# Up projection of a hybrid decoder layer: four split weights before the last operands, and the first step's products ordered by half of the tokens

## The chip, the cores and the metric

The kernel runs on one core of a Trainium2 chip. The metric is device time in microseconds (us) of one execution. The engines are named as in the profile: PE is TensorE (PEld its weight loads), DVE is VectorE, ACT is ScalarE, POOL is GpSimd and SP is SyncE; ACT, POOL and SP also issue the transfers of their own DMA queues. A row of the timeline gives the start in us from the start of the span, the duration, the engine, the line of the kernel, the operation, output<-inputs and the shape; in brackets stands the idle time of the engine before it and what ended that.

## The reference, cut to what matters

One layer: two mixers (retention, and windowed attention with sinks) on a common input projection, an output projection with a residual, and a squared-ReLU MLP with a residual. All of it is float32.

```python
D_MODEL = 1024
D_FF = 4 * D_MODEL
def rms_norm(x, gain=None):
    xf = x.astype(jnp.float32)
    y = xf * lax.rsqrt(jnp.mean(xf * xf, axis=-1, keepdims=True) + EPS)
    if gain is not None:
        y = y * gain.astype(jnp.float32)
    return y.astype(x.dtype)
```

There are 1024 prompt tokens and 8 x 8 decode tokens, 1088 in all. The change lies where the output projection ends and the MLP's first product, `rms_norm(y, gain) @ w_up`, begins; the norm's factor of each token is left out of the product and multiplied in afterwards, ahead of the square.

## The kernel before, in words

**Tokens and numbers.** The 1088 tokens stand in two superchunks s = 0, 1 of two halves of Q = 272 columns. A float32 number is split into a high part (a cast by ACT, L754) and a low part (source less high part, a subtraction by DVE, L755). A product of two split matrices is three matmuls (`mm3`, L177 to L180): high by high (L178), low weight by high operand (L179), high weight by low operand (L180). PE works in the order in which its instructions are written, and so do the other engines.

**Products.** The up projection goes in 16 steps `up(fp)`. Each step is a 2 x 2 block product by seven multiplications, in the order `PROD = (1, 2, 6, 5, 7, 4, 3)`. Product i needs a weight `w_i` and an operand, for each superchunk: 12 matmuls of 128 x 272 for each pair (i, s), so 24 for a product. Weights 1, 2 and 4 are pieces of the raw weights, weights 5, 6, 7 and 3 are sums that POOL makes (`comb`, L971). In the rows `op0` is the operand of product 1, `op1` of product 2, `op3` of 5, `op4` of 6, `op5` of 7, `op6` of 4 and `op2` of 3; `op4_1h` is the high part of product 6's operand for superchunk 1. The profile leaves such numbers out: there `op_1h` is the high part of any operand of superchunk 1, `wu_w` any split weight, `wu_s` any sum and `wu_r` any raw half. The results go to PSUM banks: products 1, 6, 7 and 4 to `psx`, 2 to `psy`, 5 and 3 to `psz`, one bank for each superchunk.

**Weights.** `left` (L961 to L981) loads the raw weights of a step as two transfers of 512 KB, `r1` and `r2`, on ACT's queue (L769) into a ring "raw" of three buffers; it yields the split weights one by one (`wsplit`), and makes the sums when it comes to a product that needs them. A transfer into a ring buffer waits until the buffer's readers are done.

**The end of the output projection.** `residual(1, m)` (L798) handles row block m of superchunk 1: POOL loads a part of the input (L800), DVE adds the two projection banks (L802), POOL stores y (L804), DVE multiplies with the gain to give f (L810), ACT squares y (L816), and DVE adds the square to the sum of squares `acc` (L817). `operands(1, m)` (L830) then makes the operands of the block: for m of 4 and above POOL makes three combinations (L845, L847, L849), and each of five operands is split by ACT and DVE. The last two blocks are m = 6 and 7. Before them the code takes the first two weights of step 0 (`ready`); so the rows of DVE and ACT hold the splits of weights 1 and 2 ahead of the operands of block 6 and 7.

**The norm of superchunk 1.** `norm(1)` (L853) sums the squares over partitions on PE (48 small matmuls into `psr`), scales them on DVE (L860, tile `nsinks`) and takes the root on POOL (L132). `norm_spread(1)` (L863) spreads the factors over partitions on PE (`psn`, L868), and ACT copies them to `rsf` (L872). In step 0 it comes after product 2 and product 6.

**After a product.** ACT copies a finished `psx` bank (L1046); after product 2 DVE adds `psy` (L1028), scales and clips (`act`, L1033), and ACT squares (L1034). A bank is written again only when its copy is done. The order of the instructions on an engine is not that of the code: a scheduler of the framework moves instructions by its own estimate of when they can run. The lists of the section on the change are the result of it.

## Time and profile before

| | |
|---|---|
| median of three runs | 1242.56 us (1240.81 to 1243.02) |
| the profiled execution's own time | 1242.26 us |
| its span, first to last instruction | 1240.5 us |
| mean granted TensorE clock | 0.983 |
| busy PE, DVE, POOL, ACT | 96%, 68%, 45%, 41% of the span |

The profiled execution has 1.8 us around its span. PE is busy nearly throughout, so what counts is where it isn't. The stage of this case lies between 525 us, where the output projection of superchunk 1 comes to its last blocks, and 572 us, where the second step of the up projection is under way. The granted clock of PE is given as a share of full speed, in ten-us stretches here.

### The profile page before, as it was taken

Reading aid. Unit: us, or ns where it says so; the run is one execution under the profiler, and the core shown is the slowest. Engines: PE = TensorE matmul, PEld = TensorE weight load, DVE = VectorE, ACT = ScalarE, POOL = GpSimd, SP = SyncE. Lnnn points to the kernel's source line nnn. Section 1 sums busy time; section 2 is a strip of 40 time slices with the busy share of each in tenths; the row PEclk is TensorE's granted clock in tenths of the full one; section 3 lists DMA queues with packets and bytes.
Section 4 is the critical chain, followed back from the end, with each engine's and each line's share of the span. In section 5 each row is a group of like instructions: output and inputs, shape, how many; then the busy total and the mean of one; then the engine's idle time right before and its main releaser. Section 6 shows DMA issues by size and latency. Waiting matters only on the chain.

```text
span 1240.5 us, 23936 instructions
## 1 busy us (share of the span) xinstructions
PE 1197.0 (96%) x9621; PEld 1150.0 (93%) x9621; DVE 849.0 (68%) x1508; ACT 507.3 (41%) x1035; POOL 557.5 (45%) x463
## 2 busy tenths in 40 slices
PE   7999999999998999969999999999899999999998
PEld 5999888888888999869999999999899999999998
DVE  7856667643136888787767666666568778897776
ACT  6343434673123435444444444444453423233331
POOL 8425333323225646467666666666662231253000
PEclk9999999999899999979999999999999999999999
DMA  6211225232415653523444444444575445643215
GB/s 236 70 59 59 88 98 165 91 101 76 120 52 183 212 163 121 164 82 125 141 141 142 151 142 150 142 151 165 178 260 162 146 150 175 202 166 126 73 55 180
DMA packets 102277, 169.46 MB, mean 137 GB/s; under 512 B 11999, under 2 KB 68255, under 8 KB 101911
## 3 DMA queue, kind: packets, MB, share of 16 engines
q1 hardware_dynamic: 88279, 123.24, 29.6%
q10 hardware_dynamic: 11328, 35.79, 8.9%
q0 software_dynamic: 2560, 8.91, 2.3%
q8 instruction: 75, 1.23, 0.4%
q14 instruction: 35, 0.29, 0.1%
HBM read 114.30 MB, written 53.61 MB: 135 GB/s over the span
## 4 chain that ended last, share of the span: by engine, by line
PE 56%; DVE 6%; DMA 2%; issue 2%; POOL 1%; ACT 1%; ACTq 0%; DVEq 0%; POOLq 0%; SPq 0%
PE psd L179 8%; PE psd L180 8%; PE psd L178 8%; PE psx L178 5%; PE psx L179 5%; PE psx L180 5%; PE psz L178 3%; PE psz L180 3%; PE psz L179 3%; PE pso L178 2%; PE pso L180 1%; PE pso L179 1%; PE psy L178 1%; PE psy L180 1%; PE psy L179 1%
## 5 line engine op out<-in xcount | busy, mean ns | idle before, releaser
L178 PE MATMUL psd<-uh,wd_w 128*128 128x272 f32 x896 | 259.5, 290 | 5.3 <-ACT a L1161 5.2
L180 PE MATMUL psd<-ul,wd_w 128*128 128x272 f32 x896 | 259.1, 290 | 2.2 <-DVE ul L755 2.2
L179 PE MATMUL psd<-uh,wd_w 128*128 128x272 f32 x896 | 260.5, 291 | 0.4 <-DVE wd_w L755 0.4
L178 PEld LDWEIGHTS psd<-uh,wd_w 128*128 128x128 f32 x896 | 170.3, 190 | 5.8 <-ACT a L1161 5.7
L180 PEld LDWEIGHTS psd<-ul,wd_w 128*128 128x128 f32 x896 | 169.7, 190 | 2.7 <-DVE ul L755 2.6
L179 PEld LDWEIGHTS psd<-uh,wd_w 128*128 128x128 f32 x896 | 169.7, 189 | 0.9 <-DVE wd_w L755 0.9
L1163 DVE TENSOR_TENSOR a<-a,psd 128x272 f32<-128x272 f32 x248 | 101.2, 429 | 41.7 <-PE psd L180 41.7
L755 DVE TENSOR_TENSOR wu_w<-wu_s,wu_w 128x512 fp32r<-128x512 f32 x64 | 58.7, 921 | 52.6 <-ACT wu_w L754 51.5
L754 ACT CAST wd_w<-wd_s 128x512 fp32r<-128x512 f32 x64 | 37.4, 619 | 118.4 <-PE psd L180 103.4
L755 DVE TENSOR_TENSOR ul<-ur,uh 128x1088 fp32r<-128x1088 f32 x56 | 81.6, 1485 | 5.6 <-ACT uh L754 5.6
L178 PE MATMUL psx<-op_0h,wu_w 128*128 128x272 f32 x256 | 74.9, 292 | 5.2 <-ACT wu_w L754 5.2
L178 PE MATMUL psx<-op_1h,wu_w 128*128 128x272 f32 x256 | 74.7, 292 | 0.0
L180 PE MATMUL psx<-op_1l,wu_w 128*128 128x272 f32 x256 | 74.6, 292 | 0.0
L180 PE MATMUL psx<-op_0l,wu_w 128*128 128x272 f32 x256 | 74.6, 292 | 0.0
L179 PE MATMUL psx<-op_0h,wu_w 128*128 128x272 f32 x256 | 74.4, 291 | 0.0
L179 PE MATMUL psx<-op_1h,wu_w 128*128 128x272 f32 x256 | 74.3, 290 | 0.0
L1033 DVE SCALAR_TENSOR_TENSOR m<-m,rsf 128x272 f32<-128x272 f32 x96 | 70.6, 736 | 4.6 <-ACT rsf L872 2.0
L366 POOL TENSOR_TENSOR sp<-sp,ssp 128x1024 f32<-128x1024 f32 (+1 forms) x16 | 28.6, 1787 | 100.4 <-DVE ssp L365 95.7
L754 ACT CAST uh<-ur 128x1088 fp32r<-128x1088 f32 x56 | 59.6, 1099 | 15.0 <-PE psd L179 9.1
L1074 POOL TENSOR_TENSOR r4t<-r3t,r4t 128x272 f32<-128x272 f32 x64 | 64.3, 1014 | 1.2
L178 PE MATMUL psf<-hnh,wqk_hi 128*128 128x384 f32 (+1 forms) x192 | 63.3, 330 | 0.0
L180 PE MATMUL psf<-hnl,wqk_hi 128*128 128x384 f32 (+1 forms) x192 | 63.1, 329 | 0.0
(328 smaller groups left out, 3797.0 us busy)
## 6 DMA issues: line engine op xcount, KB each, us to landing
ur<-u_d SPq DMA_DIRECT2D x52, 544.0 KB, 4.9
u_d<-r4t SPq DMA_DIRECT2D x32, 544.0 KB, 4.6
wu_r<-in_w_up ACTq DMA_DIRECT2D x32, 512.0 KB, 4.2
wd_r<-in_w_down ACTq DMA_DIRECT2D x30, 512.0 KB, 5.6
u_d<-r3t SPq DMA_DIRECT2D x32, 408.0 KB, 3.0
y<-in_xY POOLq DMA_DIRECT2D x16, 272.0 KB, 3.2
y_d<-y POOLq DMA_DIRECT2D x16, 272.0 KB, 3.6
yt<-y_d SPq DMA_DIRECT2D x16, 272.0 KB, 3.6
```

The source lines that it names most:

```text
L178: nc.tensor.matmul(ps, lh, rh, start=first, stop=False, skip_group_check=more)
L179: nc.tensor.matmul(ps, ll, rh, start=False, stop=False, skip_group_check=more)
L180: nc.tensor.matmul(ps, lh, rl, start=False, stop=last, skip_group_check=more)
L366: nc.gpsimd.tensor_tensor(s, s, ss.unsqueeze(2).broadcast_to([P, 4, n]), ALU.mult)
L754: nc.scalar.copy(hi, src)
L755: lo_eng.tensor_tensor(lo, src, hi.bitcast(F32), ALU.subtract)
L1033: nc.vector.scalar_tensor_tensor(t_, src, 0.0, rsf[:, s, h, :], ALU.max, ALU.mult)
L1074: sub = lambda o_, p_, q_: nc.gpsimd.tensor_tensor(o_, p_, q_, ALU.subtract)
L1163: nc.vector.tensor_tensor(to, to, ps, ALU.add)
```

## The change

Four things are changed, all at the passage from the output projection to the up projection.

1. The two sums for weights 5 and 6 of step 0 are made before the last two row blocks, in a buffer `wu0_s56` of the ring "raw", not in the pool of sums. Four weights (1, 2, 6, 5) are taken ahead of the last operands, not two; weights 6 and 5 go to other buffers (tag "wa").
2. `residual` no longer adds up the squares itself: it returns a function that does it, and for superchunk 1 this is called after the operands of the block.
3. Step 0 works its first products in the order 1 and 1 (for s = 0 and 1), then 2, 6, 5 for s = 0, then 2, 6, 5 for s = 1; the later products stay.
4. `norm(1)` is called after product 5 of s = 0, and `norm_spread(1)` after product 5 of s = 1, its matmuls behind that product's last matmul by `issue_after`. For superchunk 0 they are bound to the output projection's last matmul so far.

The diff, without the lines of `up` that are only indented in another way:

```diff
     def mm3(ps, lh, ll, rh, rl, first, last, more=False):
...
-        nc.tensor.matmul(ps, lh, rl, start=False, stop=last, skip_group_check=more)
+        return nc.tensor.matmul(ps, lh, rl, start=False, stop=last, skip_group_check=more)
...
         nc.vector.tensor_scalar(f, y, g_ffn[:, m : m + 1], None, ALU.mult)
-        if m == 0:
-            acc[s] = mw.tile([P, 2, Q], F32, tag="acc", name=f"acc{s}")
-            nc.scalar.activation(acc[s], y, AF.Square)
-        else:
-            sq = om.tile([P, 2, Q], F32, tag="sq", name=f"sq{s}_{m}")
-            nc.scalar.activation(sq, y, AF.Square)
-            nc.vector.tensor_tensor(acc[s], acc[s], sq, ALU.add)
+
+        def squares():
+            if m == 0:
+                acc[s] = mw.tile([P, 2, Q], F32, tag="acc", name=f"acc{s}")
+                nc.scalar.activation(acc[s], y, AF.Square)
+            else:
+                sq = om.tile([P, 2, Q], F32, tag="sq", name=f"sq{s}_{m}")
+                nc.scalar.activation(sq, y, AF.Square)
+                nc.vector.tensor_tensor(acc[s], acc[s], sq, ALU.add)
+
+        return squares
...
-    def norm_spread(s):
+    def norm_spread(s, ins):
...
+                with tc.issue_after(ins.ins):
+                    nc.tensor.matmul(
...
         if ms == (6, 7):
-            gen0 = left(PROD, a["w_up"][0], "wu0", nc.vector, tags=("wa", "wa", "wb", "wb"))
-            ready = [next(gen0), next(gen0)]
+            r0 = [rawload(a["w_up"][0][:, i * 1024 : i * 1024 + 1024], f"wu0_r{i + 1}") for i in range(2)]
+            s56 = mw.tile([P, 1024], F32, tag="raw", name="wu0_s56", bufs=3)
+            nc.gpsimd.tensor_tensor(s56[:, :512], r0[1][:, :512], r0[1][:, 512:], ALU.add)
+            nc.gpsimd.tensor_tensor(s56[:, 512:], s56[:, :512], r0[0][:, :512], ALU.subtract)
+            gen0 = left(
+                PROD, None, "wu0", nc.vector, tags=("wa", "wa", "wa", "wa", "wb", "wb", "wb"), raws=r0,
+                sums={5: s56[:, :512], 6: s56[:, 512:]})
+            ready = [next(gen0) for _ in range(4)]
         for m in ms:
-            residual(1, m, [pss[m, h] for h in range(2)])
+            squares = residual(1, m, [pss[m, h] for h in range(2)])
             if rest:
                 operands(0, rest.pop(0))
             operands(1, m)
+            squares()
...
-            norm_spread(0)
+            norm_spread(0, last_out[0])
...
+        order = [(i, s) for i in PROD for s in range(2)]
+        if fp == 0:
+
+            order = [(1, 0), (1, 1), (2, 0), (6, 0), (5, 0)] + [(i, 1) for i in (2, 6, 5)] + order[8:]
...
-        for i in PROD:
-            w = next(gen)
-            for s in range(2):
+        for i, s in order:
+            if i not in ws:
+                ws[i] = next(gen)
+            w = ws[i]
...
                 if i == 2:
                     t_ = add(1, s, bk)
                     wait.append((t_, t_, s, 0, ra[s][:, B11, :]))
                     if fp or s == 0:
                         act(*wait.pop())
-                    else:
-                        norm(1)
-                if i == 6 and s == 1 and wait:
-                    norm_spread(1)
+            if fp == 0 and (i, s) == (5, 0):
+                norm(1)
+            if fp == 0 and (i, s) == (5, 1):
+                norm_spread(1, mm)
...
```

How it moves the instructions is seen in the lists of an engine's instructions in program order. The names carry the number of the step, the superchunk and a running number: `psy1_6067` is the bank of product 2 for superchunk 1, `wu0_w6` is weight 6 of step 0.

**PE, from the second half of product 1 to product 7 of step 0, before** (the first rows of each run of matmuls into a bank; a run has 12 where nothing else is said):

```order
L178 MATMUL psy0_6066<-op1_0h_5292,wu0_w2_6007 128x272
...
L178 MATMUL psy1_6067<-op1_1h_5466,wu0_w2_6007 128x272
...
L158 MATMUL psr1_6130<-ones_69,acc1_5541 32x1 x24
...
L178 MATMUL psx0_6064<-op4_0h_5294,wu0_w6_6161 128x272
L178 MATMUL psx1_6065<-op4_1h_5468,wu0_w6_6161 128x272
...
L178 MATMUL psz0_6068<-op3_0h_5296,wu0_w5_6202 128x272
...
L178 MATMUL psz1_6069<-op3_1h_5470,wu0_w5_6202 128x272
...
L178 MATMUL psx0_6064<-op5_0h_5298,wu0_w7_6231 128x272
```

and now:

```order
L178 MATMUL psy0_6075<-op1_0h_5292,wu0_w2_6010 128x272
...
L178 MATMUL psz0_6077<-op3_0h_5296,wu0_w5_6016 128x272
...
L158 MATMUL psr1_6152<-ones_69,acc1_5551 32x1 x24
...
L178 MATMUL psy1_6076<-op1_1h_5466,wu0_w2_6010 128x272
...
L178 MATMUL psz1_6078<-op3_1h_5470,wu0_w5_6016 128x272
...
L178 MATMUL psx0_6073<-op4_0h_5294,wu0_w6_6013 128x272
...
L178 MATMUL psx1_6074<-op4_1h_5468,wu0_w6_6013 128x272
...
L178 MATMUL psx0_6073<-op5_0h_5298,wu0_w7_6230 128x272
L178 MATMUL psx0_6351<-op0_0h_5290,wu1_w1_6365 128x272
L178 MATMUL psx1_6352<-op0_1h_5464,wu1_w1_6365 128x272
L179 MATMUL psx0_6351<-op0_0h_5290,wu1_w1_6365 128x272
L178 MATMUL psx1_6074<-op5_1h_5472,wu0_w7_6230 128x272
```

The scheduler has put product 5 ahead of product 6, so weight 5, which the code takes after weight 6, is the first new one that PE asks for. Superchunk 1's product 2, which needs the last operands, has moved behind it. Between the two halves of product 7 now stand three matmuls of the next step's product 1 (`psx0_6351`, `psx1_6352`); before, that product's first matmul stood behind both halves. From the next step's product 2 on, PE's order is the same in both kernels, after 192 matmuls of the up projection in each.

**POOL, from the last combination of block 4 to the last one of block 5, before:**

```order
L849 TENSOR_TENSOR f1_4_5833<-f1_4_5833,f1_0_5539 128x272
L800 DMA y1_6_6010<-in_xY 128x544
L804 DMA y_d_130<-y1_5_5851 128x2x272
L845 TENSOR_TENSOR f1_1_5558<-f1_5_5856,f1_1_5558 128x272
L847 TENSOR_TENSOR f1_1_5558<-f1_5_5856,f1_1_5558 128x272
L849 TENSOR_TENSOR f1_5_5856<-f1_5_5856,f1_1_5558 128x272
```

and now:

```order
L853 TENSOR_TENSOR f1_4_5833<-f1_4_5833,f1_0_5539 128x272
L1004 TENSOR_TENSOR wu0_s56_6004<-wu0_r2_6002 128x512
L800 DMA y1_6_6019<-in_xY 128x544
L804 DMA y_d_130<-y1_5_5851 128x2x272
L849 TENSOR_TENSOR f1_1_5558<-f1_5_5856,f1_1_5558 128x272
L851 TENSOR_TENSOR f1_1_5558<-f1_5_5856,f1_1_5558 128x272
L1005 TENSOR_TENSOR wu0_s56_6004<-wu0_s56_6004,wu0_r1_6000 128x512
L853 TENSOR_TENSOR f1_5_5856<-f1_5_5856,f1_1_5558 128x272
```

The first sum stands ahead of the load for block 6, the second one between the second and the third combination of block 5. Before, both stood behind the last combination of block 7. Line 849 of the changed kernel is L845 of the kernel before.

**ACT, where the first raw load of the next step stands, before:**

```order
L754 CAST op4_1h_5468<-f1_0_5539 128x272
L769 DMA wu1_r1_6362<-in_w_up 128x1024
L754 CAST op5_1h_5472<-f1_0_5539 128x272
L816 ACTIVATE sq1_5_5858<-y1_5_5851 128x544
```

and now, some thirty instructions further on:

```order
L1050 ACTIVATE r3t0_0_6079<-m10_0_6095 128x272
L754 CAST wu0_w3_6306<-wu0_s3_6304 128x512
L769 DMA wu1_r1_6361<-in_w_up 128x1024
L769 DMA wu1_r2_6363<-in_w_up 128x1024
L769 DMA wu2_r1_6622<-in_w_up 128x1024
L1063 COPY m60_0_6138<-psx0_6073 128x272
L754 CAST wu1_w1_6365<-wu1_r1_6361 128x512
```

The sums hold the ring's third buffer, so the next step's first raw half has to wait for a buffer until the weights of step 0 are read. Its load stands behind the square of the first result (`r3t`) and the cast of weight 3, with the two loads that follow it. On DVE the splits of weights 6 and 5 now stand between the operand splits of block 6 (the one after the product with the gain, the other after the split of `op4` for block 6), and the adds to `acc` stay in between.

More of the change, by code (lines that the diff above doesn't have):

```diff
@@ L770, in rawload @@
         return raw
-    mix, acc, fs = {}, {}, {}
+    mix, acc, fs, last_out = {}, {}, {}, [None]
     def mix_load(s, pl):
@@ L795, in out_half @@
             mh, ml = (mix[s, half + x][:, k, h, :] for x in "hl")
-            mm3(ps, lh, ll, mh, ml, first and k == 0, last and k == 3)
+            last_out[0] = mm3(ps, lh, ll, mh, ml, first and k == 0, last and k == 3)
     def residual(s, m, pss):
@@ L867, in norm_spread @@
             for i, (c0, n) in enumerate(((0, 128), (128, 128), (256, 16))):
-                nc.tensor.matmul(
-                    pb[:, c0 : c0 + n], rf[:, 3 * h + i : 3 * h + i + 1].broadcast_to([P, 128]), ident[:, 128 - n :],
-                    start=True, stop=True,
-                )
+                with tc.issue_after(ins.ins):
+                    nc.tensor.matmul(
+                        pb[:, c0 : c0 + n], rf[:, 3 * h + i : 3 * h + i + 1].broadcast_to([P, 128]), ident[:, 128 - n :],
+                        start=True, stop=True,
+                    )
             nc.scalar.copy(rsf[:, s, h, :], pb[:, :Q])
@@ L918, in out_early @@
             out_half(0, "r", pss[h], h, wr_, False, True)
-        residual(0, m, pss)
+        residual(0, m, pss)()
     gens, ahead = {}, []
@@ new lines, in up @@
+        for i, s in order:
+            if i not in ws:
+                ws[i] = next(gen)
+            w = ws[i]
+            bk, first = home[i][0][s], home[i][1]
+            for k in range(4):
+                lh, ll = (w[:, j, k * 128 : k * 128 + 128] for j in range(2))
+                rh, rl = (ops[RIGHT[i]][s][j][:, k, :] for j in range(2))
+                mm = mm3(bk, lh, ll, rh, rl, first and k == 0, k == 3, not first)
+            if i in (1, 6, 7):
+                t_ = held[i, s] = tq(f"m{i}", s)
+                nc.scalar.copy(t_, bk)
+            if i == 2:
+                t_ = add(1, s, bk)
+                wait.append((t_, t_, s, 0, ra[s][:, B11, :]))
+                if fp or s == 0:
+                    act(*wait.pop())
+            if fp == 0 and (i, s) == (5, 0):
+                norm(1)
+            if fp == 0 and (i, s) == (5, 1):
+                norm_spread(1, mm)
+            if i == 7:
+                if wait:
+                    act(*wait.pop())
+                t_ = add(7, s, z[s])
+                act(t_, t_, s, 1, ra[s][:, B22, :])
+            if i == 4:
+                act(tq("v", s), bk, s, 0, ra[s][:, B21, :])
+                nc.sync.dma_start(u_d[fp // 2][:, fp % 2, s, :3, :], ra[s])
+            if fp == 15 and s == 1 and i == 2:
+                first_down(1, ("1h", "1l", "2h", "2l"))()
+            if fp == 15 and s == 1 and i == 5:
+                split6.append(first_down(6, ("6h", "6l", "5h", "5l")))
+            if i == 3:
+                t_ = add(6, s, bk)
+                r12 = um.tile([P, Q], F32, tag="r12", name=f"r12{fp}_{s}", bufs=2)
+                ins = act(t_, t_, s, 1, r12)
+                b11, b21, b22 = (ra[s][:, i_, :] for i_ in (B11, B21, B22))
+                t1, t2, t3, t4 = (rb[s][:, i_, :] for i_ in range(4))
+                sub = lambda o_, p_, q_: nc.gpsimd.tensor_tensor(o_, p_, q_, ALU.subtract)
+                sub(t1, r12, b11)
+                sub(t2, b22, t1)
+                sub(t4, b21, t2)
+                sub(t3, b22, r12)
+                nc.sync.dma_start(u_d[fp // 2][:, fp % 2, s, 3:, :], rb[s])
```

39 lines of the change are left out of this document (1 added, 38 removed).

## The prediction

> **What bounds the kernel now.** The page's first part and the waits of PE between 480 and 640 us come first (who was waited for: us in total, times, longest), then PE by ten-us stretches (busy time of PE, PEld, DVE, ACT, POOL with counts; granted clock, share and GB/s of the transfers).
>
> ```profile
> PE 1197.0 (96%) x9621; PEld 1150.0 (93%) x9621; DVE 849.0 (68%) x1508; ACT 507.3 (41%) x1035; POOL 557.5 (45%) x463
> ...
> PE psx L178 <- ACT wu_w L754: 5.2, 1, 5.2
> PE psy L180 <- DVE op_1l L755: 3.5, 2, 2.0
> ...
> PE psy L178 <- ACT op_1h L754: 1.7, 1, 1.7
> ...
> 530.00:540.00 10.00, 6.29 (x47) 5.87 (x46) 9.05 (x16) 5.58 (x13) 6.81 (x10) 0.90 0.26 88
> 540.00:550.00 10.00, 3.28 (x56) 2.41 (x56) 9.07 (x13) 4.28 (x11) 8.68 (x8) 0.50 0.07 23
> 550.00:560.00 10.00, 10.00 (x65) 10.00 (x64) 6.19 (x9) 4.72 (x11) 4.86 (x5) 0.75 0.27 106
> ```
>
> PE fills 96% of the span, but here it waits 10.4 us (5.2 + 3.5 + 1.7), while DVE is 90% busy. PE's timeline shows the places:
>
> ```profile
> 529.85 0.28 PE L178 MATMUL psx<-op_0h,wu_w 128*128 128x272 f32 x1
> 529.97 0.29 PE L179 MATMUL psx<-op_0h,wu_w 128*128 128x272 f32 x1
> ...
> 535.26 0.28 PE L179 MATMUL psy<-op_1h,wu_w 128*128 128x272 f32 x1
> 537.51 0.39 PE L180 MATMUL psy<-op_1l,wu_w 128*128 128x272 f32 x1 [1.96 <-DVE op_1l L755]
> 539.64 0.59 PE L178 MATMUL psy<-op_1h,wu_w 128*128 128x272 f32 x1 [1.75 <-ACT op_1h L754]
> 542.03 0.59 PE L180 MATMUL psy<-op_1l,wu_w 128*128 128x272 f32 x1 [1.56 <-DVE op_1l L755]
> 542.55 0.82 PE L158 MATMUL psr<-ones,acc 128*32 128x1 f32 x48
> 548.53 0.59 PE L178 MATMUL psx<-op_0h,wu_w 128*128 128x272 f32 x1 [5.16 <-ACT wu_w L754]
> ...
> 553.05 0.43 PE L178 MATMUL psx<-op_1h,wu_w 128*128 128x272 f32 x1
> 553.28 0.43 PE L179 MATMUL psx<-op_1h,wu_w 128*128 128x272 f32 x1
> ...
> 554.41 1.68 PE L868 MATMUL psn<-c_ident,nsinks 128*128 128x128 f32 x12
> ...
> 571.16 0.29 PE L178 MATMUL psy<-op_0h,wu_w 128*128 128x272 f32 x1
> ```
>
> From 529.85 to 535.26 lie 43 matmul starts, 0.126 us each. Then product 2 of superchunk 1 waits three times for the last operands, and product 6 for its weight. At the granted 0.50 a matmul takes 0.227 (553.05 to 553.28); the full clock is back about 555, some 6.5 us after PE set in again (the stretch from 550 has 0.75 on average). The last row is the next step's product 2. From there PE's order is the same in both kernels and no wait follows up to 640 us, so I read the change's worth as the shift of this row. It stands 192 up matmuls after 529.85 in both.
>
> **The change part by part.** DVE and POOL set the pace, and they get in each other's way (their timelines):
>
> ```profile
> 525.89 0.43 DVE L755 TENSOR_TENSOR op_1l<-f,op_1h 128x272 fp32r<-128x272 f32 x1
> ...
> 528.70 0.68 DVE L755 TENSOR_TENSOR wu_w<-wu_r,wu_w 128x512 fp32r<-128x512 f32 x1
> 530.50 0.56 DVE L755 TENSOR_TENSOR op_1l<-f,op_1h 128x272 fp32r<-128x272 f32 x1 [1.12 <-ACT op_1h L754]
> ...
> 534.41 2.34 DVE L817 TENSOR_TENSOR acc<-acc,sq 128x544 f32<-128x544 f32 x1 [0.24 <-ACT sq L816]
> ...
> 538.65 0.49 DVE L810 TENSOR_SCALAR f<-y,c_g_ffn 128x544 f32<-128x544 f32 x1
> ...
> 539.41 1.29 DVE L817 TENSOR_TENSOR acc<-acc,sq 128x544 f32<-128x544 f32 x1
> 540.63 5.45 DVE L755 TENSOR_TENSOR op_1l<-f,op_1h 128x272 fp32r<-128x272 f32 x6
> 546.00 0.77 DVE L1028 TENSOR_TENSOR m<-m,psy 128x272 f32<-128x272 f32 x2
> 546.70 0.81 DVE L1033 SCALAR_TENSOR_TENSOR m<-m,rsf 128x272 f32<-128x272 f32 x1
> ```
>
> ```profile
> 524.58 0.77 POOL L849 TENSOR_TENSOR f<-f,f 128x272 f32<-128x272 f32 x1
> 527.53 0.56 POOL L800 DMA_DIRECT2D y<-in_xY  x1 [2.18 <-DMA y_d<-y]
> ...
> 528.82 1.19 POOL L845 TENSOR_TENSOR f<-f,f 128x272 f32<-128x272 f32 x1
> ...
> 534.67 0.78 POOL L845 TENSOR_TENSOR f<-f,f 128x272 f32<-128x272 f32 x1
> 535.41 0.75 POOL L847 TENSOR_TENSOR f<-f,f 128x272 f32<-128x272 f32 x1
> ...
> 544.44 1.34 POOL L971 TENSOR_TENSOR wu_s<-wu_s,wu_r 128x512 f32<-128x512 f32 x1
> ```
>
> A low split alone takes 0.43 us; six of them beside POOL's sums take 5.45, 0.91 each. So a DVE operation with two inputs in SBUF and a POOL operation take turns, each delayed by what is left of the other. The 2.34 at 534.41 is more: it ends behind two POOL operations.
>
> *First sum.* It fits POOL's gap of 2.18 us: 525.35 + about 1.34 = 526.7, before the load at 527.53, so POOL isn't later. But the low split of 525.89 stands beside it, and DVE falls back 0.55. The three splits behind it and the low half of weight 1 then come after POOL's 528.82 and not before: they take turns with it and with the combination that follows. Before, the low half of weight 1 ended at 529.38; with the 0.55 and two POOL turns of 0.77, a part of the first being over (1.2 together, an estimate), it ends at 531.1. PE asks for it at 529.97: **+1.1 us**, a new stall.
>
> *Weights 5 and 6 early, product 5 first.* From 531.1 PE has 35 matmuls ahead, product 1 twice and 2 once, 4.4 us: it asks for weight 5 at 535.5. In ACT's list its high half stands behind block 6's third cast, which waits for POOL. Before, its combination ended at 535.45 (534.67 + 0.78); DVE's delay of 1.7 moves it, since it needs block 6's f from DVE, and a cast of 0.55 follows: 537.7, idle 2.2. That the second sum (1.34) delays POOL as well is no more than DVE's own delay and is not added. Up to the low half, DVE has 15 operations behind weight 1's: ten of 272 columns at 0.35 (546.00 to 546.70 for two), three low halves of weights, the gain, and one addition to `acc`, 6.4 us in all, and about 2.7 behind POOL, two combinations of 0.77 and the second sum less an overlap: 531.1 + 9.1 = 540.2, idle 2.4 to 2.5. Together **+4.6** in place of 1.96 + 1.75 + 1.56 = 5.27.
>
> *The wait of 5.16 goes.* At 540.2 weights 2, 6 and 5 are all there. PE runs eleven matmuls of 5, psr, 2 and 5 of superchunk 1, 6 twice, psn and the first half of 7: 71 matmuls. In 6.5 us at half clock go psr (0.8) and 25 of them at 0.227; 46 at 0.126 are 5.8, psn 1.2 (1.53 at the half clock, from 554.41): through at 553.7. The half clock costs nothing as long as the next term ends later.
>
> *The next step's load.* It is the price of the ring buffer (ACT's timeline, POOL's first sum of the next step, and the landings of the raw halves over the whole trace):
>
> ```profile
> 523.94 0.34 ACTq L769 DMA_DIRECT2D wu_r<-in_w_up  x1
> ...
> 547.54 0.43 ACT L1034 ACTIVATE r3t<-m 128x272 f32<-128x272 f32 x1 [3.58 <-DVE m L1033]
> 547.88 1.64 ACT L754 CAST wu_w<-wu_s 128x512 fp32r<-128x512 f32 x3
> ...
> 552.13 0.33 ACTq L769 DMA_DIRECT2D wu_r<-in_w_up  x1
> ...
> 555.40 1.28 POOL L971 TENSOR_TENSOR wu_s<-wu_r 128x512 f32<-128x512 f32 x1 [5.06 <-DMA wu_r<-in_w_up]
> ...
> DMA to landing us min/median/max: 3.1/4.2/6.8
> ```
>
> Before it went out at 523.94 and nothing waited. Now it stands behind the square `r3t`, which waits for DVE, and the cast of weight 3. On DVE block 7's f stands right behind weight 5's low half: 540.2 in place of 538.65, and the same eight operations follow. The last low split ended at 546.08 and now ends at 547.6. Then nsinks 0.1, the add 0.35 and the scale 0.8 to 1.3 (0.81 at 546.70, more beside POOL): 549.3; `r3t` 0.34 (547.54 to 547.88) and the cast 0.55: the load goes out at **550.2**. Behind it on ACT stand two more loads and the copy of product 6's bank; PE's product 7 waits for that copy, which is done within the 1.6 us of idling below. It lands 3.3 later (the row of 552.13 has 3.1 to POOL's start at 555.40; the median of all is 4.2), and the cast of its first half ends at 554.1 to 554.5, DVE's low half at 555.3. PE, through at 553.7, stands at the next step's product 1, of which three matmuls come before the second half of product 7: **idle to 555.3**, 1.6 us.
>
> From there 82 matmuls are left to product 2 (192 less nine half products and two): 10.3 us. One more wait: product 4 writes over the bank of product 7, whose copy stands on ACT behind a second `r3t`, which waits for DVE's scale behind the low half of the next step's second weight: 0.68 and 0.81 after 555.3, `r3t` and the copy 0.7, and parts of two POOL sums in the way, 1.5 by my estimate: 3.7, less the 21 matmuls that PE has until then, 2.6: about 1.1. So 555.3 + 10.3 + 1.1 = **566.7**, against 571.16: -4.4 us.
>
> **Which price of a collision.** The row of 534.41 is 2.34 where its sister at 539.41 is 1.29: a POOL operation that starts after it, and a second, both got ahead. One repeat of it (1.05), or a load at the median landing of 4.2 (0.9), on this chain moves the end that far. I take one of them, 0.9: -3.5.
>
> [...]
>
> **The rivals.**
>
> *The gain is eaten, no difference.* The three loads stand one behind another on the queue, in one burst of 1.5 MB; the worst of the landings is 6.8. At 6.8, 3.5 later than in the sum, the next step's weight 1 comes at 558.8 and the end at about 570: -1.0, 1241.3 us. For it: POOL's 5.06 idle before 555.40 is a load that is waited for even when it has little beside it. Against: the stretch of 540 to 550 moves 23 GB/s and the queue is free.
>
> *Slower: POOL twice ahead of DVE.* In the new list POOL has eleven operations from the first sum to block 7's last combination, each beside a DVE operation of two inputs. If the 2.34 is the rule and not the exception, each such meeting costs up to 1.05 more, and all lie on the chain to 550.2: eight more make +8.0, less 3.5: +4.5, 1246.8. It turns the sign from four more on. Against it: the six of 5.45, at 0.91 each, are not like this.
>
> *Larger gain.* If the collisions of the added sums cost nothing (the second can fall into DVE's own wait of 1.12 us ahead of 530.50), f of block 7 goes back to 538.65 and the load to 548.7; with no POOL sum in the copy's way either the end is 555.3 - 1.55 + 10.3 = 564.1, -7.1, 1235.2.
>
> *The change does not do what it says.* The code asks for 2, 6, 5; the list shows 5 ahead of 6. My sum is made by the list. With 6 first, as the code has it, PE would begin earlier with weight 6, whose low half DVE makes seven operations before weight 5's, but the load of 550.2 hangs on DVE alone and would set the same end: 1238.8 as well, so it is no case of its own.
>
> **How the numbers follow.** The profiled execution has 1242.26, within 0.3 of the median 1242.56: 1242.26 - 3.5 = 1238.8. Forecast 0.60, no difference 0.22, larger gain 0.10, slower 0.08. The forecast's own bounds are -5.0 and -2.0, 1237.3 to 1240.3; with half of the larger gain and most of the case of no difference the range is 1236.0 to 1242.0. A measurement tells about 0.2%, 2.5 us, from no change: faster means below 1240.1. The forecast is below it in nine of ten (0.54) and the larger gain always (0.10); no difference has 0.22 and the rest of the forecast 0.05; slower 0.09.
>
> **What would show it.** Right: PE's waits in this stage are about 1.1 for weight 1, 2 to 2.5 twice for weight 5, and 1 to 3 for the next step's weight 1, whose releaser is ACT and behind it the load; no wait for weight 6; the load goes out at 550 and lands 3 to 4 later; product 2 of the next step starts near 567. Wrong: the load out before 548 (the chain of DVE is shorter) or after 552 (POOL gets ahead more often), a wait of PE later than 572, or a wait for operand splits of superchunk 1, which the sum has at nothing.

## The result and the profile after

The changed kernel takes 1236.21 us (median of 14 runs, 1232.2 to 1240.18) where the kernel before takes 1242.1 (14 runs, 1239.63 to 1243.15). The ratio is 0.995 with a 95% interval of 0.994 to 0.9961, that is 4.8 to 7.5 us faster. The forecast was 1238.8, 3.5 us faster. The sign and the chain of waits came out as forecast. The gain is larger, mainly because one term of the sum was too long.

The first profile of the changed kernel fell on the longest of its 14 runs (1240.18 us, span 1238.4), only 2.1 below the profiled execution of before. So both kernels were profiled once more (labels c0 for the kernel before, e0 for the changed one, spans 1241.3 and 1234.9), and the reading goes by stretches, not by whole spans. **The stretch** below runs from DVE's addition to y of block 5, superchunk 1 (the row of L802 that waits for y's load) to the first matmul of the next step's product 2, the row by which the prediction sums.

| execution | block 5's addition | next step's product 2 | the stretch |
|---|---|---|---|
| before | 525.18 | 571.16 | 45.98 |
| before, again (c0) | 525.96 | 571.64 | 45.68 |
| change | 528.80 | 569.16 | 40.36 |
| change, again (e0) | 525.65 | 566.00 | 40.35 |

The stretch is 5.3 to 5.6 us shorter and repeats within 0.3 us, while its begin differs by 3.2 us between two executions of the same changed kernel. That begin is decided earlier in the program.

The page's first part of the changed kernel, and PE's waits between 515 and 625 us:

```profile
span 1238.4 us, 23936 instructions
PE 1200.2 (97%) x9621; PEld 1152.2 (93%) x9621; DVE 855.1 (69%) x1508; ACT 506.8 (41%) x1035; POOL 557.0 (45%) x463
```

```profile
PE psx L179 <- DVE wu_w L755: 3.0, 2, 2.8
PE psx L178 <- ACT m L1063: 1.1, 3, 0.5
PE psr L158 <- DVE acc L819: 0.3, 1, 0.3
```

The waits for the last operands and the 5.2 for weight 6 are gone. 10.4 us of waiting have become 4.4, most of it for the low half of weight 1. PE's timeline shows where:

```profile
537.07 0.59 PE L179 MATMUL psx<-op_0h,wu_w 128*128 128x272 f32 x1 [2.82 <-DVE wu_w L755]
...
546.61 0.58 PE L158 MATMUL psr<-ones,acc 128*32 128x1 f32 x48 [0.33 <-DVE acc L819]
...
555.29 0.39 PE L178 MATMUL psx<-op_0h,wu_w 128*128 128x272 f32 x1 [0.23 <-ACT m L1063]
...
557.90 0.39 PE L179 MATMUL psx<-op_0h,wu_w 128*128 128x272 f32 x1 [0.21 <-DVE wu_w L755]
...
569.16 0.29 PE L178 MATMUL psy<-op_0h,wu_w 128*128 128x272 f32 x1
```

The row of 546.61 is the simplest account of the gain. PE's sums of squares (psr) need block 7's addition to `acc`, and they start 17.81 us after block 5's addition (546.61 - 528.80); before it was 17.37 (542.55 - 525.18), and in both kernels 48 matmuls of product work lie ahead of them. So up to there the change gains nothing. From there to the last row PE has the same work in both, and it takes 22.55 us in place of 28.61: the wait of 5.16 is gone, and so is the half clock behind it. The ten-us stretches (columns as in the prediction):

```profile
530.00:540.00 10.00, 7.18 (x47) 6.97 (x47) 10.00 (x16) 4.94 (x12) 6.20 (x9) 0.81 0.27 84
540.00:550.00 10.00, 9.58 (x107) 9.12 (x107) 9.58 (x16) 5.27 (x14) 8.82 (x9) 0.85 0.17 57
550.00:560.00 10.00, 9.30 (x70) 8.55 (x69) 7.76 (x12) 4.64 (x11) 5.16 (x5) 1.00 0.44 157
```

In 540 to 550 us PE starts 107 matmuls where it started 56 (48 of them are the small ones of psr, in both). The granted clock is 0.85 there where it had 0.50, and 1.00 in the next ten us where it had 0.75. DVE is busy 9.58 to 10.00 of ten: it sets the pace, as before. DVE's, POOL's and ACT's timelines give the chain to the next step's load (`wu_s` in POOL's rows of L1004 and L1005 are the two early sums):

```profile
528.80 0.79 DVE L802 TENSOR_TENSOR y<-pso,y 128x272 f32<-128x272 f32 x2 [2.27 <-DMA y<-in_xY]
...
531.23 3.58 DVE L819 TENSOR_TENSOR acc<-acc,sq 128x544 f32<-128x544 f32 x1
...
535.78 1.24 DVE L755 TENSOR_TENSOR wu_w<-wu_r,wu_w 128x512 fp32r<-128x512 f32 x1
...
543.37 1.20 DVE L755 TENSOR_TENSOR wu_w<-wu_s,wu_w 128x512 fp32r<-128x512 f32 x1
544.49 0.49 DVE L810 TENSOR_SCALAR f<-y,c_g_ffn 128x544 f32<-128x544 f32 x1
...
546.48 5.53 DVE L755 TENSOR_TENSOR op_1l<-f,op_1h 128x272 fp32r<-128x272 f32 x6
...
552.46 0.44 DVE L1049 SCALAR_TENSOR_TENSOR m<-m,rsf 128x272 f32<-128x272 f32 x1
```

```profile
528.92 1.28 POOL L1004 TENSOR_TENSOR wu_s<-wu_r 128x512 f32<-128x512 f32 x1
...
531.45 0.79 POOL L849 TENSOR_TENSOR f<-f,f 128x272 f32<-128x272 f32 x1
532.18 0.78 POOL L851 TENSOR_TENSOR f<-f,f 128x272 f32<-128x272 f32 x1
532.91 1.30 POOL L1005 TENSOR_TENSOR wu_s<-wu_s,wu_r 128x512 f32<-128x512 f32 x1
```

```profile
552.93 0.43 ACT L1050 ACTIVATE r3t<-m 128x272 f32<-128x272 f32 x1 [0.27 <-DVE m L1049]
552.94 0.33 ACTq L769 DMA_DIRECT2D wu_r<-in_w_up  x1
553.27 0.60 ACT L754 CAST wu_w<-wu_s 128x512 fp32r<-128x512 f32 x1
...
556.50 1.14 ACT L754 CAST wu_w<-wu_r 128x512 fp32r<-128x512 f32 x2 [1.26 <-DMA wu_r<-in_w_up]
```

Block 5's addition to `acc` takes 3.58 us in place of 0.72: it stands behind three POOL operations in a row, the last of them the second early sum. That delay is about as long as PE's wait of 2.82, though c0 below shows that such a wait can come without it. And the load goes out 0.01 us after `r3t` has started and 0.33 us before the cast of weight 3 starts (553.27), not behind both of them.

### The profile page after: what moved, and what is told of

Its sections match the earlier page's. It is cut to its first block, busy times and chain, and to the rows that moved or that the text cites. A ratio compares the mean times of both kernels' runs of the same rounds, so it can differ in the third digit from the quotient of the medians.

```text
span 1238.4 us, 23936 instructions
## 1 busy us (share of the span) xinstructions
PE 1200.2 (97%) x9621; PEld 1152.2 (93%) x9621; DVE 855.1 (69%) x1508; ACT 506.8 (41%) x1035; POOL 557.0 (45%) x463
## 4 chain that ended last, share of the span: by engine, by line
PE 53%; DVE 7%; DMA 2%; issue 2%; POOL 2%; ACT 1%; ACTq 0%; DVEq 0%; POOLq 0%
PE psd L179 8%; PE psd L180 8%; PE psd L178 7%; PE psx L178 5%; PE psx L180 4%; PE psx L179 4%; PE psz L178 2%; PE psz L180 2%; PE psz L179 2%; PE pso L178 2%; PE pso L180 2%; PE pso L179 1%; DVE ul L755 1%; DVE op_0l L755 1%; PE psy L178 1%
## 5 line engine op out<-in xcount | busy, mean ns | idle before, releaser
L755 DVE TENSOR_TENSOR wu_w<-wu_s,wu_w 128x512 fp32r<-128x512 f32 x64 | 64.5, 1008 | 50.1 <-ACT wu_w L754 49.3
L366 POOL TENSOR_TENSOR sp<-sp,ssp 128x1024 f32<-128x1024 f32 (+1 forms) x16 | 28.6, 1788 | 100.4 <-DVE ssp L365 95.6
L755 DVE TENSOR_TENSOR wd_w<-wd_s,wd_w 128x512 fp32r<-128x512 f32 x64 | 55.0, 872 | 13.9 <-ACT wd_w L754 13.6
```

The costliest lines, as they stand in the source:

```text
L366: nc.gpsimd.tensor_tensor(s, s, ss.unsqueeze(2).broadcast_to([P, 4, n]), ALU.mult)
L755: lo_eng.tensor_tensor(lo, src, hi.bitcast(F32), ALU.subtract)
```

## The experiments

Each is a change of the changed kernel, except c0. Every ratio is against runs of the kernel before on the same chip.

**The change once more** (no edit).

> The changed kernel once more, for a second look at its stage. Theory A (the spread of its times, 1232 to 1240, is made in this stage: DVE's additions and splits fall behind one, two or three POOL operations by chance): the wait for weight 1's low half and the start of the load of the next step lie elsewhere than in the first profile by 1 us or more, relative to the start of the up projection. Rival B (the spread comes from before the stage): these stand within 0.5 us relative to block 5's gain, and the start of the up projection has moved. Time 1234 to 1239.

Measured: 1236.83 us, ratio 0.9958 (0.9945 to 0.9971). PE's timeline:

```profile
534.03 0.39 PE L179 MATMUL psx<-op_0h,wu_w 128*128 128x272 f32 x1 [2.24 <-DVE wu_w L755]
...
540.33 0.39 PE L178 MATMUL psz<-op_0h,wu_w 128*128 128x272 f32 x1 [1.63 <-ACT wu_w L754]
...
541.54 0.39 PE L179 MATMUL psz<-op_0h,wu_w 128*128 128x272 f32 x1 [0.83 <-DVE wu_w L755]
...
543.53 0.58 PE L158 MATMUL psr<-ones,acc 128*32 128x1 f32 x48 [0.33 <-DVE acc L819]
...
554.74 0.39 PE L179 MATMUL psx<-op_0h,wu_w 128*128 128x272 f32 x1 [0.21 <-DVE wu_w L755]
...
566.00 0.29 PE L178 MATMUL psy<-op_0h,wu_w 128*128 128x272 f32 x1
```

Here PE does wait for weight 5 (1.63 + 0.83). In the first profile it did not, where a lower clock (0.81 and 0.85) used that time up. The stretch is the same to 0.01, as DVE's chain is the same: `acc` of block 5 has 3.56, psr starts 17.88 after block 5's addition, the load 24.21 (24.14 in the first). The span is 3.5 shorter than the first one's, and 3.15 of that is there when block 5's addition starts (525.65 against 528.80).

**The kernel before once more** (no edit).

> The kernel before once more, for a second look at its stage. From the first matmul behind 503.6 us of the first trace to the one behind 616.9 the first profile has 113.3 us, the change has 109.4 and 108.4 in its two profiles. Theory A (the stage of before is steady, and its first profile typical): 112.5 to 114 for the same matmuls, and its wait at the begin of the down projection is 4.3, as in the other runs, or 5.2 as in its first profile; 4.3 would say that the 0.9 us there is no effect of the change. Rival (the first profile was slow in this stage): under 112. Time 1240 to 1243.

Measured: 1242.66 us, ratio 0.9999 (0.9986 to 1.0013). A row of PE's timeline and three of DVE's:

```profile
532.50 0.39 PE L179 MATMUL psx<-op_0h,wu_w 128*128 128x272 f32 x1 [3.06 <-DVE wu_w L755]
```

```profile
527.78 1.30 DVE L817 TENSOR_TENSOR acc<-acc,sq 128x544 f32<-128x544 f32 x1
529.01 2.26 DVE L755 TENSOR_TENSOR op_1l<-f,op_1h 128x272 fp32r<-128x272 f32 x3
531.20 1.25 DVE L755 TENSOR_TENSOR wu_w<-wu_r,wu_w 128x512 fp32r<-128x512 f32 x1
```

The kernel before can also wait for weight 1, 3.06 us, where its first profile had no wait there. DVE's five operations meet POOL's combinations (4.7 us from the begin of the first to the end of the last, 527.78 to 532.45; 2.4 in the first profile, 527.00 to 529.38). POOL begins them 2.40 us after block 5's addition here (528.36), 3.64 in the first profile (528.82): its load ahead of them waits for a transfer that comes sooner or later, and begins 1.02 us after the addition here (526.98), 2.35 in the first profile (527.53). So the wait for weight 1 isn't the price of the change alone, and its size before was one draw.

**The order alone.** Step 0's sums and weights as before, the new order of products kept:

> The new product order, the new places of the norm and of the squares, with two weights ahead and the sums at their old place. Theory A (the early weights make the gain, the order alone can do nothing as weight 6 comes when it came): PE waits for weight 6 or 5 in one piece of 12 to 15 us, and product 2 of superchunk 1 is done after it: 1241 to 1245. Rival (the order makes the gain, since PE no longer waits for the last operands): no wait of over 6 us, 1236 to 1239.

```diff
-            r0 = [rawload(a["w_up"][0][:, i * 1024 : i * 1024 + 1024], f"wu0_r{i + 1}") for i in range(2)]
...
-            ready = [next(gen0) for _ in range(4)]
+            gen0 = left(PROD, a["w_up"][0], "wu0", nc.vector, tags=("wa", "wa", "wb", "wb"))
+            ready = [next(gen0), next(gen0)]
```

```profile
552.45 0.59 PE L178 MATMUL psx<-op_0h,wu_w 128*128 128x272 f32 x1 [12.53 <-ACT wu_w L754]
```

Measured: 1242.76 us, ratio 1.001 (0.9995 to 1.0024). All that PE waited in pieces before stands now in one wait of 12.53 for weight 6 (beside 1.24 for weight 1), and the stretch is 47.51 (its profile is of the longest of its 12 runs, 1247.18). The order brings nothing while the weights are late.

**The weights alone.** Early sums and four weights ahead, but the old order of products, with the calls of the norm at the places that fit it:

> The four early weights with their sums in the ring and the late squares, with the old product order (1, 2, 6 each for both halves) and the norm after product 2 and its spreading after product 6. Theory A: the three waits of product 2 stay (about 6 us with the first stall of weight 1), the wait for weight 6 is gone, and as the next step's product 1 now stands behind product 3, its late load is hidden: 1235 to 1239, as the whole change. Rival (the order is needed): 1240 to 1243.

```diff
-            order = [(1, 0), (1, 1), (2, 0), (6, 0), (5, 0)] + [(i, 1) for i in (2, 6, 5)] + order[8:]
+            pass
...
-            if fp == 0 and (i, s) == (5, 0):
+            if fp == 0 and (i, s) == (2, 1):
                 norm(1)
-            if fp == 0 and (i, s) == (5, 1):
+            if fp == 0 and (i, s) == (6, 1):
                 norm_spread(1, mm)
```

Measured: 1238.31 us, ratio 0.997 (0.9955 to 0.9984), stretch 41.17. The weights make most of the gain: 3.2 of the 4.7 us that e0 gains on the same chip (before: 1241.52). With them the order adds 0.8 us in the stretch and 1.5 in the medians (1238.31 to 1236.83), while the two intervals overlap: likely, not shown.

**No sums on POOL.** The buffer of the sums is filled by a load; weights 5, 6 and 3 of step 0 are then other numbers, and the two additions are left out:

> The changed kernel without its two early POOL sums: the ring buffer is filled by a third transfer, so the values for weights 5, 6 and 3 of step 0 are others (this part of the computation is left out), and all splits and the ring's occupation stay. Theory A (the sums hold up DVE, by about 1.2 to 2.5 us up to block 7's gain): the stall for weight 1 shrinks from 2.8 to under 1, the next step's load goes out 1.3 to 2.5 earlier, 1233 to 1235. Rival (collisions cost nothing in the end): 1236 to 1237.

```diff
-            s56 = mw.tile([P, 1024], F32, tag="raw", name="wu0_s56", bufs=3)
-            nc.gpsimd.tensor_tensor(s56[:, :512], r0[1][:, :512], r0[1][:, 512:], ALU.add)
-            nc.gpsimd.tensor_tensor(s56[:, 512:], s56[:, :512], r0[0][:, :512], ALU.subtract)
+            s56 = rawload(a["w_up"][1][:, :1024], "wu0_s56")
```

DVE's timeline and PE's:

```profile
526.57 0.72 DVE L819 TENSOR_TENSOR acc<-acc,sq 128x544 f32<-128x544 f32 x1
527.21 1.14 DVE L755 TENSOR_TENSOR op_1l<-f,op_1h 128x272 fp32r<-128x272 f32 x3
```

```profile
529.00 0.40 PE L179 MATMUL psx<-op_0h,wu_w 128*128 128x272 f32 x1 [0.18 <-DVE wu_w L755]
...
536.02 0.39 PE L178 MATMUL psz<-op_0h,wu_w 128*128 128x272 f32 x1 [2.18 <-ACT wu_w L754]
...
538.43 0.59 PE L179 MATMUL psz<-op_0h,wu_w 128*128 128x272 f32 x1 [2.02 <-DVE wu_w L755]
```

Measured: 1234.2 us, ratio 0.994 (0.9919 to 0.996), stretch 39.07. The sums cost 1.3 us of the stretch, by one execution each; the medians differ by 2.6, with overlapping intervals. Up to the next step's load they cost more: it goes out 21.91 us after block 5's addition in place of 24.21. Behind the waits for weight 5 the granted clock is 0.63 in this execution (15 to 25 us after block 5's addition) where e0 has 1.00, and that may take a part back. The wait for weight 1 is gone and that for weight 5 has come (4.2 in all): DVE is late for PE in any case, the collision decides at which weight PE stands. In this execution POOL's combinations began late (3.62 us after block 5's addition), as in the first profile of before, so a part of the 1.3 can be that.

**Product 5 second.** For the waits on weight 5 of e0, products in the order 1, 5, 2, 6, weights 1, 5, 2, 6 (`norm(1)` and `norm_spread(1)` are then called after product 6 of s = 0 and of s = 1):

> The change with weight 5 split ahead of weights 2 and 6, and product 5 for both halves of the tokens right behind product 1 (its operands are complete by then, block 3 at the latest). Theory A (the late load of the next step sets the end; PE's waits for weight 5 are a second chain that ends at about the same time): the waits for weight 5 shrink from 2.4 to under 1, PE then waits longer for the next step's weight 1: 0 to -1 against the change, 1235.5 to 1237. Rival (PE's own waits set the end): -2 to -3, 1233.5 to 1235.

```diff
-                PROD, None, "wu0", nc.vector, tags=("wa", "wa", "wa", "wa", "wb", "wb", "wb"), raws=r0,
+                (1, 5, 2, 6, 7, 4, 3), None, "wu0", nc.vector, tags=("wa", "wa", "wa", "wa", "wb", "wb", "wb"), raws=r0,
...
-            order = [(1, 0), (1, 1), (2, 0), (6, 0), (5, 0)] + [(i, 1) for i in (2, 6, 5)] + order[8:]
+            order = [(1, 0), (1, 1), (5, 0), (5, 1), (2, 0), (6, 0), (2, 1), (6, 1)] + order[8:]
```

A row of PE's timeline and one of ACT's:

```profile
546.76 0.60 PE L178 MATMUL psx<-op_0h,wu_w 128*128 128x272 f32 x1 [2.60 <-ACT m L1063]
```

```profile
546.33 0.66 ACT L1063 COPY m<-psx 128x272 f32<-128x272 f32 x2
```

Measured: 1237.54 us, ratio 0.9947 (0.9928 to 0.9966), stretch 42.09. The waits on weight 5 are gone, and product 6 now waits 2.60: it writes over product 1's bank, whose copy stands on ACT behind all operand casts. In the order of the change product 5 goes to another bank (psz) and lies over that time.

**The next step's load early.** The term that the prediction called the price of the ring: the first raw half goes to a free buffer of the weights (their tags are dealt out so that one is free) and is issued behind the last operand cast, at 542.46, 19.5 us after block 5's addition and not 24.2:

> The change with the next step's first raw half loaded into a free weight buffer, so that it doesn't wait for the ring; it goes out behind the last cast of the operands, some 3.5 us earlier; weight 3 of step 0 goes to another buffer. Theory A: the next step's waits (0.3 and the copies' 1.0) go, PE's own waits then set the end: -0.5 to -1.3 against the change, 1235 to 1236. Rival (the load alone sets the end): -2.5 to -3.5, 1233 to 1234.

```diff
...
+            raws=(early1[0], rawload(a["w_up"][1][:, 1024:], "wu1_r2")) if fp == 1 else None)
+        if fp == 0:
+            early1.append(mid.tile([P, 1024], F32, tag="wb", name="wu1_r1", bufs=4))
+            nc.scalar.dma_start(early1[0], a["w_up"][1][:, :1024])
```

```profile
542.46 0.33 ACTq L1036 DMA_DIRECT2D wu_r<-in_w_up  x1
```

Measured: 1235.67 us, ratio 0.9934 (0.9917 to 0.9952), stretch 38.45. This is the lowest of the versions that compute all, but its interval overlaps that of the change (0.994 to 0.9961), and its profile is of the fastest of its six runs (1233.08). PE's rows of psr and of the stretch's end:

```profile
540.22 0.58 PE L158 MATMUL psr<-ones,acc 128*32 128x1 f32 x48 [0.32 <-DVE acc L819]
...
561.39 0.29 PE L178 MATMUL psy<-op_0h,wu_w 128*128 128x272 f32 x1
```

From psr to the end it takes 21.17 us, where e0 takes 22.47 (543.53 to 566.00), both at a granted clock of 1.00: 1.3 us less. The edit also moves POOL's sum for weight 7 behind block 7's last six splits on DVE, which take 3.34 in place of 5.53 here, so the 1.3 is not the load's alone.

**Early load with other orders.** The same early load with product 5 second (e7), with the second sum later (e9), and with the old order (e12); the second sum later without it (e8); both sums later with it (e11). The later sum stands behind the last combination of block 5:

```diff
-            nc.gpsimd.tensor_tensor(f[:, 0, :], f[:, 0, :], t1, ALU.subtract)
+            last_comb[0] = nc.gpsimd.tensor_tensor(f[:, 0, :], f[:, 0, :], t1, ALU.subtract)
...
-            nc.gpsimd.tensor_tensor(s56[:, 512:], s56[:, :512], r0[0][:, :512], ALU.subtract)
+            with tc.issue_after(last_comb[0].ins):
+                nc.gpsimd.tensor_tensor(s56[:, 512:], s56[:, :512], r0[0][:, :512], ALU.subtract)
```

(In e11 it stands around the first sum, and the second follows it.)

> Product 5 second and the early load together. Theory A (two chains that end together: only both shortened bring the whole): -2.5 to -4 against the change, 1232.5 to 1234.5. Rival (one of the two chains is the bound and the other has slack): no more than the better of the two alone, within 0.7 us.

> The change with its second POOL sum put behind block 5's last combination (before, between the second and the third). Theory A (the addition or the splits of DVE fall behind a row of POOL operations without a gap, and the second sum lengthens that row from 1.5 to 2.8 us: 3.58 and 3.56 us in the two profiles of the change): the longest DVE operation of block 5 is at most 2.4, the wait for weight 1's low half falls from 2.2 to 2.8 to under 1.5, the stage from the matmul at 503.6 to the one at 616.9 takes 107 to 108 us in place of 109.4 and 108.4, and the time is -0.7 to -1.5 against the change. Rival (the row of three is chance and not made by the sum): the wait stays above 2 and the time within 0.5.

> The second sum behind block 5's last combination and the next step's first raw half loaded into a free weight buffer, as in the run with the early load. Theory A (with both, neither weight 1 nor the late load holds PE): stage of 106 to 107.5 us, time 1233 to 1235 beside a before of 1242 to 1243. Rival (DVE's operand splits then end last, and they aren't touched): as the early load alone, 108.3 for the stage, 1235.5.

> Both sums behind block 5's last combination, and the early load. Theory A (POOL idles there before block 6's store, some 1.5 to 2.3 us, so one of the sums is nearly free, and block 5's splits run as without sums): the wait for weight 1's low half under 0.5 us as in the run without sums, the wait for weight 5 0.5 to 1 longer; stage of 105.5 to 107 us, 1232.5 to 1234.5. Rival (the sums hold up block 6's combinations by as much): as with only the second sum moved, within 0.7 us.

> The four early weights and the early load of the next step, with the old product order and places of the norm. From block 5's first addition on DVE to the next step's product 2 on PE the run with the early load and the new order took 38.4 us, the early weights alone 41.2, the change 40.4. Theory A (with the load out of the way the new order is worth what PE waits for the last operands under the old one): 40 to 41.5 us for that stretch, and 1 to 2 us longer in time than with the new order, 1236.5 to 1238.5. Rival (the order is worth nothing, the weights and the load are all): 38 to 39.

In the table the fourth column is the time from block 5's addition to the first matmul with weight 1's low half on PE, and the last one the granted clock from 15 to 25 us after block 5's addition.

| kernel | us | ratio (95%) | weight 1's low half | the stretch | clock |
|---|---|---|---|---|---|
| e0, the change | 1236.83 | 0.9958 (0.9945 to 0.9971) | 8.38 | 40.35 | 1.00 |
| e6, early load | 1235.67 | 0.9934 (0.9917 to 0.9952) | 7.75 | 38.45 | 1.00 |
| e5, product 5 second | 1237.54 | 0.9947 (0.9928 to 0.9966) | 8.58 | 42.09 | 0.75 |
| e7, and early load | 1237.09 | 0.9949 (0.9931 to 0.9967) | 8.27 | 41.82 | 0.74 |
| e8, second sum later | 1236.06 | 0.9943 (0.9922 to 0.9964) | 7.34 | 40.61 | 0.66 |
| e9, and early load | 1236.84 | 0.9947 (0.9929 to 0.9966) | 7.03 | 42.26 | 0.50 |
| e2, old order | 1238.31 | 0.997 (0.9955 to 0.9984) | 7.73 | 41.17 | 0.83 |
| e12, and early load | 1237.77 | 0.9963 (0.9949 to 0.9977) | 8.37 | 41.88 | 0.66 |
| e11, both sums later, early load | 1237.23 | 0.9953 (0.9936 to 0.997) | 6.57 | 43.04 | 0.54 |

In four pairs the early load changes the stretch by -1.9, -0.3, +1.7 and +0.7 us. Weight 1's low half, for which PE waits in all eight runs, comes 0.6 and 0.3 us earlier, 0.3 earlier and 0.6 later: that is the whole of the second and of the fourth pair. Left are 1.3 us less from e0 to e6, and 2.0 more from e8 to e9. The ten us from 15 to 25 us after block 5's addition, in e6, e8 and e9:

```profile
537.94:547.94 10.00, 8.58 (x108) 8.12 (x108) 9.93 (x18) 6.17 (x16) 7.88 (x7) 1.00 0.32 109
536.66:546.66 10.00, 8.89 (x90) 8.63 (x91) 8.53 (x18) 5.62 (x13) 9.20 (x8) 0.66 0.09 30
538.04:548.04 10.00, 9.21 (x84) 8.94 (x85) 8.49 (x16) 5.43 (x13) 8.67 (x7) 0.50 0.24 82
```

From e0 to e6 the clock is 1.00 on both sides; from e8 to e9 it falls from 0.66 to 0.50. So the late load seems to hold the changed kernel by about a microsecond where PE has its full clock; where it has not, PE is late itself and the early load brought nothing. This is argued from one execution of each kernel, and what makes the clock fall in one and not in another is not shown. e7, e9 and e11 stayed behind what was expected of them (1232.5 to 1235 us), and e7 and e9 are slower than the early load alone.

e8 and e11 answer on the sums. DVE's timeline of e8:

```profile
524.19 0.71 DVE L819 TENSOR_TENSOR acc<-acc,sq 128x544 f32<-128x544 f32 x1
524.83 2.95 DVE L755 TENSOR_TENSOR op_1l<-f,op_1h 128x272 fp32r<-128x272 f32 x3
527.71 1.24 DVE L755 TENSOR_TENSOR wu_w<-wu_r,wu_w 128x512 fp32r<-128x512 f32 x1
```

With the second sum moved away the addition to `acc` is free (0.71), and the splits behind it pay (2.95 in place of 1.14, 1.24 in place of 0.68). In all, weight 1's low half comes 1.0 us earlier than in e0 (7.34 and 8.38). PE, which starts the up projection earlier here too (4.56 us after block 5's addition, in e0 5.85), still waits 2.5 for it, and weight 5 costs 1.55 + 2.15. With both sums later (e11) PE, which starts at 6.21, has next to no wait for weight 1, 0.59 for weight 2, and weight 5 costs 2.18 + 3.11. So the place of the sums shifts DVE's delay from one weight to the next and does not save it: psr starts 17.88 us after block 5's addition in e0, 18.90 in e8 and 20.59 in e11, and 16.47 without sums (e4). In these runs POOL's work between block 5 and block 7 took DVE's time wherever it stood. None of these versions beats the change beyond the intervals.

## Why the prediction was right and where it was wrong

Its chain, counted from block 5's addition on DVE, against both profiles of the change:

| term | predicted | change | e0 |
|---|---|---|---|
| block 7's f on DVE | 15.0 | 15.69 | 15.76 |
| from f to the issue of the next step's load | 10.0 | 8.45 | 8.45 |
| from issue to the low half of weight 1 on PE | 5.1 | 4.96 | 4.88 |
| from there to product 2 | 11.4 | 11.26 | 11.26 |
| sum | 41.5 | 40.36 | 40.35 |

**The step that failed** is "The next step's load", by its size: it has the load go out behind the scale of 0.8 to 1.3 us, `r3t` of 0.34 and the cast of 0.55. The scale took 0.44, the load went out as `r3t` began (552.93 and 552.94; in e0 549.85 and 549.86), and so the term is 8.45 and not 10.0. At which point of ACT's work a queued load starts was taken for granted there, and not read from a row. With that, PE waits 0.21 us at the next step's first weight (and 0.23 ahead of it, at product 7, for a copy on ACT) and not 1.6. PE's arrival there is near the forecast, 28.6 us after block 5's addition against 28.5, but by two misses that cancel: weight 5's low half came 0.8 later than in the sum, and the half clock behind psr did not come. That the load is still a part of what sets the end, e6 bears out: with the load 4.7 us earlier the time from psr to the end is 1.3 shorter at the same clock.

**The added 0.9.** One collision beyond the sum was allowed for, and one came, at `acc` of block 5 (3.58 and 3.56). But the 0.7 in the table's first row is what is left of two misses that go against each other. Weight 1's low half ends on DVE 8.2 and 8.3 us after block 5's addition, not 5.9; from there to the end of weight 5's low half DVE takes 7.5, not 9.1. That their sum came near the allowance is luck. So the stage's -5.6 against the forecast's -3.5 is about 1.55 from the load, 0.2 of the allowance and 0.3 of the last two terms.

**The first sum** was placed rightly, in POOL's gap (it starts 0.12 after block 5's addition; predicted 0.17). The new stall at weight 1 was put at 1.1 and measured 2.82 and 2.24: the sum took POOL's combinations at the 3.64 us of the first profile, and they came at 2.65 and 2.76, and so beside `acc` and not behind it. c0 shows that the kernel before meets the same (2.40, wait 3.06).

**Weights 5 and 6.** 4.6 of waiting for weight 5 was right in kind: 2.46 in e0, nothing in the first profile, 4.2 where weight 1 costs nothing (e4). Together with weight 1 it was 5.7 predicted, 2.8 and 4.7 measured. The shift between the two weights was missed; it moves nothing, as DVE sets the end. That no wait for weight 6 would be left, and none for operand splits of superchunk 1, was right.

**The half clock** behind psr, 6.5 us of it, came in neither profile of the change. The 0.81 and 0.85 of the first one lie ahead of psr, behind the stall for weight 1; from 544 to 554 us it has 1.00, and e0 has 1.00 from 530 on. The low clock ahead of psr cost nothing in the stretch, which is the same without it. That a half clock behind psr costs nothing beside the late load, e8 bears out: at a clock of 0.66 it takes 21.71 us from psr to the end, and e0 at 1.00 takes 22.47.

**The rivals.** Slower by POOL getting ahead more often: the 2.34 is not the exception (3.58, 3.56, 4.14 for the three splits of e5), but it happened at one place of the stage and not at eight, and in c0 as well. A late landing: the low half of weight 1 followed the issue by 4.96 and 4.88, near the sum. The larger gain had -7.1 from collisions that cost nothing; the sums cost 1.3 of the stretch (e4), and what the gain has beyond the forecast came for the most part from the load's term. That the product order in the list differs from the code's was given no weight; no run has the code's order with the early weights.

**From the stretch to the span.** The start of the same matmul of PE's list, less block 5's addition: at 616.93 us of before 91.75 (c0 91.46), in the change 86.88 and 86.58. So 0.5 to 0.7 of the 5.6 is given back in the next steps. Later PE waits 5.2 and 6.5 for the first operand of the down projection in the two profiles of before, and 4.3 and 4.4 in those of the change; but e1, whose weights come as before, has 4.3 too. Why that wait is shorter stays open, and with it 1 us of the measured 5.9. What the fourth part of the change does for superchunk 0, ahead of the stage, no run isolates: block 5's addition stands between 521.66 and 528.80 us in the profiles of the change and its variants, and at 525.18 and 525.96 in those of before.

## What to carry to other kernels

Weights ahead of the last operands paid here, where the tensor engine stood still at a change of stages (10.4 us of waits before, 4.4 after); the order of the products alone did not (ratio 1.001), since the same work stayed late on the engine that makes the weights. Sum such a stage on the engine that sets its pace, from one anchor row on that engine, and compare stretches between anchors: two executions of one kernel differed here by 3.2 us before the stage began, and in the stretch by 0.01. Read the granted clock of a stretch beside its length before a difference is put down to an edit. And ask of a queued load at which row of its engine it starts, not only behind which.

## What the runs showed of the hardware

**A DVE operation can be passed by several POOL operations in a row.** 0.72 us became 3.58 and 3.56 beside three POOL operations of 0.79, 0.78 and 1.30 in the first profile, all of which started after it (531.45, 532.18 and 532.91 against 531.23). Three splits of 1.14 together became 2.95 (e8) and 4.14 (e5). In the prediction the two take turns, each delayed by what is left of the other. One split fits that: it took 1.01 in place of 0.43 beside POOL's first sum (529.50 in the first profile of the change; the sum of 1.28 began at 528.92). The rows above differ from it. The two additions of L802 at 528.80, each with one input in a PSUM bank, took 0.79 together beside the same sum, and 0.77 at 538.25 with no POOL operation beside them. Which of the two goes first when both have a queue, the rows show only for these cases.

**A load can go out while an activation ahead of it on ACT's list still runs, and before the next one starts.** The next step's load went out 0.01 us behind the start of `r3t` in both profiles of the change (552.93 and 552.94, 549.85 and 549.86) and did not wait for its 0.43 us. By ACT's list the cast of weight 3 stands between the two, and it started 0.33 us after the load (553.27, 550.19).

**The clock falls around a wait of about 3 us in some executions only.** Ahead of the stage PE waits for the same addition to y in every profile: 2.90 and 3.07 us in the two of before, 2.88 and 2.85 in the two of the change. PE's timeline has it so in c0 and then in the change:

```profile
508.14 0.39 PE L178 MATMUL pso<-mixah,woa 128*128 128x272 f32 x1 [3.07 <-DVE y L802]
```

```profile
511.43 0.39 PE L178 MATMUL pso<-mixah,woa 128*128 128x272 f32 x1 [2.88 <-DVE y L802]
```

The ten us around and behind it, in the same order and then of e0:

```profile
510.00:520.00 10.00, 10.00 (x84) 10.00 (x83) 8.66 (x16) 5.11 (x11) 5.05 (x6) 1.00 0.67 214
```

```profile
510.00:520.00 10.00, 8.57 (x56) 8.57 (x57) 6.83 (x13) 2.77 (x6) 4.69 (x6) 0.83 0.42 134
```

```profile
510.00:520.00 10.00, 10.00 (x75) 10.00 (x74) 8.35 (x15) 4.62 (x9) 5.87 (x7) 0.88 0.57 176
```

The granted clock is 1.00 in both profiles of before, 0.83 and 0.88 in those of the change, behind waits that differ by 0.2 us and are not longer where the clock fell. Over all fourteen profiles, those of the experiments included, the clock of the ten us behind this wait is 0.83 in six, with waits of 2.85 to 3.14 us, and 1.00 in eight, with waits of 2.90 to 3.15. In the stage it is the same: behind the stall of 2.82 the clock was 0.81 and 0.85, behind that of 2.24 it stayed at 1.00. What makes it fall is not shown. A fall that comes in one execution and not in the next may be a part of the 8 us between the fastest and the slowest run of the same kernel (1232.2 and 1240.18 us); that is argued and not shown.
